# First key and value projections of a two-layer diffusion trunk: which engine makes the low weight parts, and in which order the opening steps stand

## The chip, the cores and the metric

The kernel runs on one core of one Trainium2 chip. A core has five engines with queues of their own: TensorE (PE in the profile, with PEld for its weight loads), VectorE (DVE), ScalarE (ACT), GpSimd (POOL) and SyncE (SP), which here issues nearly all DMA transfers. Engines wait for each other through semaphores; each works its own queue in order. The metric is the device time of one execution in microseconds (us), as the median of several runs.

## The reference

Two trunk layers work on 512 latent tokens of width 1024, with 256 context tokens beside them. What the change touches is the very beginning of layer 0:

```python
sh1, sc1, g1, sh2, sc2, g2 = adaln_params(c, mod_w[i], mod_b[i])         # silu(c) @ w + bias
h  = modulate(rms_norm(x,   norm_g[i, 0]), sh1,  sc1)                    # h * (1 + scale) + shift
hc = modulate(rms_norm(ctx, norm_g[i, 0]), csh1, csc1)
proj = h @ w_in                                                          # queries, keys and values
k_ac, v_ac, k_bc, v_bc = split_kv(hc @ w_in[:, Q_WIDTH:])
```

After that come global and windowed attention, a gated feed-forward part with a width-3 convolution, and a second layer with Fourier mixing in place of attention. All of it is float32.

## The kernel before, in words

**Products.** A float32 product is made of three faster ones. Every operand is split into a high part (a rounded copy, by ACT) and a low part (the operand less its high part), and `mm3` (lines 103 to 107) adds high times high (line 104), high times low (line 105) and low times high (line 106). `split` (line 126) makes the two parts of a weight; ACT's copy and the subtraction both carry line 127. In `split` the engine of the subtraction is an argument, VectorE if none is given.

**The opening.** The first 512 columns of the key and value weights (`w_kva`) are multiplied with all tokens: four latent token tiles and two context tiles of 128, each with an accumulator of its own. The width of 1024 is cut into eight chunks `c` of 128. For each chunk three things must be there before its products: the shift and scale of these 128 features (an adaLN tile), the split weights of the chunk, and the normalised tokens.

**The steps.** The order in which the code writes these steps is a string, `START` (line 60), which a loop walks through. Its letters are:

- `Mc`, `mod_tile(c)` (line 664): eight small float32 products with the adaLN weights of chunk c (line 672), ACT's copy of the sums (line 675), two transposes by TensorE (line 679), and three small VectorE steps (lines 681, 683, 685) that leave shift (`modc`) and scale (`derc`). The weights of all eight tiles are loaded by SP early on, into buffers that later hold other things (`yT`, `K`, `V` and a `raw` buffer).
- `Wc`, `weights(c)` (line 744): the split of the key and value weights of chunk c, 128x512 each. Two chunks share a load (`raw<-in_w_kva`, line 136) and a pair of buffers `wh`, `wl`. Before the change it passes GpSimd to `split`.
- `Xi` and `Y2`: sums of squares for the second half of the latent tokens (two parts) and for the context tokens (line 698 on VectorE, line 700 on ACT, products at line 187). `bcast` and `R2` (line 233) spread the reciprocal roots over the partitions; those of the second token half go inside `M2`.
- `Fci`, `feed(c, i)` (line 711): modulates chunk c of token set i (0 and 1 are the halves of the latent tokens, 2 is the context) and multiplies it with the weights, two token tiles with three products each. VectorE makes `md_t` (line 250), ACT the high part `hh` or `ch` (line 251), VectorE the low part `hl` or `cl` (line 252).
- `B0`, and part of `F01`: products by `busy` (line 179, product at line 181) whose result nobody reads. How many is set by the list `HOT` (line 56). In `F01` (lines 725 to 739) the products are written out on lines 737, 738 and 740, with `HOT[2]` busy products ahead of them and `HOT[3]` between their two parts.

**Who sets the order.** The string gives the order of the code; a scheduler with priorities then decides the order on each engine, so instructions of neighbouring steps are mixed. Weight loads share three `raw` buffers: SP may issue the next load into a buffer only when the low part made from it is done.

**What follows.** Three groups of further projections (`group_weights`, 128x1024 splits on VectorE, lines 104 to 106 with 128x256 results) run while VectorE and GpSimd normalise and rotate the keys and VectorE sums up two more adaLN rows (line 521). Then attention begins.

Of the kernel before, what the change touches and what calls it, by code (L numbers as in the profile page):

```python
# [10 lines left out]
F32 = mybir.dt.float32  # L11
# [41 lines left out]
SIDE = 16  # L53

WARM = 36
HOT = [5, 8, 5, 6]
HOT2 = [2, 2, 2]


START = ("M0 W0 X0 M1 B0 W1 F00 X1 F10 M2 W2 M3 F01 F11 F20 W3 F21 M4 Y2 F30 F31 R2 F02 W4 F12 F22 F32 M5 W5 F40 "  # L60
         "F41 M6 F42 W6 F50 F52 W7 F60 M7 F62 F51 F61 F70 F71 F72")

FILL = [[1, 0, 1, 2, 1, 1, 1, 1],
# [18 lines left out]
def kernel(ctx: ExitStack, tc: tile.TileContext, a):  # L82
    nc = tc.nc
    V, S, G, PE, SY = nc.vector, nc.scalar, nc.gpsimd, nc.tensor, nc.sync
# [15 lines left out]
    def f(ap):  # L100
        return ap.bitcast(F32)
# [19 lines left out]
    def held(i):  # L121
        if i.ins.engine in fences:
            tc.add_manual_dep(i.ins, fences[i.ins.engine], mybir.DependencyInfo(
                mybir.DependencyClass.NoSync, mybir.DependencyReason.DATA), reason="fence")

    def split(h, l, src, eng=V):
        i = S.copy(out=h, in_=src), eng.tensor_tensor(out=l, in0=src, in1=f(h), op=ALU.subtract)  # L127
        for j in i:
            held(j)
# [9 lines left out]
    def wpair(shape):  # L139
        return mk(wp, shape, F32R, "wh", 5), mk(wp, shape, F32R, "wl", 5)  # L140
# [35 lines left out]
    W4 = HT // 4  # L176


    def busy(ps, src, n):
        for _ in range(n):  # L180
            PE.matmul(ps[:32, :src.shape[1]], lhsT=ones32, rhs=src, start=True, stop=True)
# [396 lines left out]
    with ExitStack() as es:  # L578
# [27 lines left out]
        with ExitStack() as e1:  # L606
# [19 lines left out]
            kva = {}  # L626
# [64 lines left out]
            def x_sums(src, n, eng=V, hot=0, ps=None, ks=range(KC)):  # L691
                if ps is None:
                    ps = mk(pps, [P, T], F32, "mm", 6)
                for k in ks:
                    sq = sqx[:, nsq[0] % 6, :]
                    nsq[0] += 1
                    if k % 2:
                        eng.tensor_tensor(out=sq[:, :n], in0=src[:, k, :], in1=src[:, k, :], op=ALU.mult)
                    else:
                        i = S.activation(out=sq[:, :n], in_=src[:, k, :], func=AF.Square)  # L700
                        if nsq[0] == 1:
                            follow(i, ahead)
                    stat_add(ps, sq, n, k == 0, k == KC - 1)
                busy(warm, sq[:, :n], hot)
                return ps
# [10 lines left out]
            def feed(c, i):  # L716
# [12 lines left out]
                if (c, i) == (0, 1):  # L729

                    busy(warm, Rs[1], HOT[2])
                    for part in range(2):
# [8 lines left out]
                        if part == 0:  # L741
                            busy(warm, f(hh[:, 0, halves[1]]), HOT[3])

            def weights(c):
                if c % 2 == 0:
                    kw[c // 2] = wpair([P, 2, T])
                wh, wl = kw[c // 2]
                split(wh[:, c % 2, :], wl[:, c % 2, :], kva[c // 2][:, c % 2, :], G)

            ps0 = x_sums(xT[:, :, halves[0]], HT, V, HOT[0])  # L750

# [6 lines left out]

            for s in START.split():
                n = [int(c) for c in s[1:]]  # L760
                if s == "M0":
                    mod_tile(0, lambda: bcast(0, ps0))
                elif s == "M2":
                    mod_tile(2, lambda: bcast(1, Rs[1]))
                elif s == "Y2":
                    r2 = rstd(x_sums(cT, TC)[:, :W4])
                elif s == "R2":
                    Rs[2] = spread(r2, pps)
                elif s == "B0":
                    busy(warm, Rs[0], HOT[1])  # L770
                else:
                    {"M": mod_tile, "W": weights, "X": sums, "F": feed}[s[0]](*n)
# [489 lines left out]
    def ffn(l, xp, ready, pre, mid, gem, plain=None):  # L1262
# [146 lines left out]
        for gi, (f0, nch) in enumerate(GROUPS[l]):  # L1409
# [42 lines left out]
            for d in range(2):  # L1452
                weights(d)
# [3 lines left out]
            for d in range(KC):  # L1457
                if d not in ws:
                    weights(d)
                part(d, hs[d], begun.get(d))  # L1460
                if gem is not None and not end:
                    pump(gem, GP[1])
# [16 lines left out]
    with ExitStack() as es:  # L1479
        up = es.enter_context(tc.tile_pool(name="up", bufs=1, reuse_waits="tile", side="right"))  # L1480
        M1 = 258
# [104 lines left out]
        def fourier_weights(d, eng=G):  # L1586
            r = f_first[d] if d < 2 else raw([P, 4, 2, P], a["w_f"][d])

            pm = (yT[:, 6:8, :] if d in (3, 5) else yT[:, 2:4, :] if d == 1 else mk(cp, [P, 2, T], F32, "gacc")).rearrange(
                "p a (g c) -> p a g c", g=4)  # L1590
            held(eng.tensor_tensor(out=pm[:, 0, :, :], in0=r[:, :, 0, :], in1=r[:, :, 1, :], op=ALU.add))
            held(V.tensor_tensor(out=pm[:, 1, :, :], in0=r[:, :, 1, :], in1=r[:, :, 0, :], op=ALU.subtract))
            wh, wl = wpair([P, 2, 4, P])
            split(wh, wl, pm)
            return wh, wl
# [40 lines left out]
        for d in range(KC):  # L1636
            wh, wl = w_f.pop() if w_f else fourier_weights(d)
# [139 lines left out]
```

## Time and profile before

| what | value |
|---|---|
| median of 3 runs | 1136.24 us (1133.64 to 1137.02) |
| profiled execution | 1138.32 us, of which 1136.5 us are its span |
| PE busy | 1098.6 us, 97% of the span |
| DVE, ACT, POOL busy | 902.6, 592.9, 174.9 us |
| DMA from 10 to 40 us | 413 to 420 GB/s, busy share 1.01 to 1.04 |

The span runs from the first to the last instruction; the execution's own time is 1.8 us longer. In the timeline a row gives start, duration, engine, line, operation, tiles and count; what stands in square brackets is the idle time of the engine ahead of the row, and what ended it. A float32 product of lines 181, 187, 672 or 679 appears as two records, so that x10 at line 181 is five products.

### The profile page before, as it was taken

Reading aid. Unit: us, or ns where it says so; the run is one execution under the profiler, and the core shown is the slowest. Engines: PE = TensorE matmul, PEld = TensorE weight load, DVE = VectorE, ACT = ScalarE, POOL = GpSimd, SP = SyncE. Lnnn points to the kernel's source line nnn. Section 1 sums busy time; section 2 is a strip of 40 time slices with the busy share of each in tenths; the row PEclk is TensorE's granted clock in tenths of the full one; section 3 lists DMA queues with packets and bytes.
Section 4 is the critical chain, followed back from the end, with each engine's and each line's share of the span. In section 5 each row is a group of like instructions: output and inputs, shape, how many; then the busy total and the mean of one; then the engine's idle time right before and its main releaser. Section 6 shows DMA issues by size and latency. Waiting matters only on the chain.

```text
span 1136.5 us, 19542 instructions
## 1 busy us (share of the span) xinstructions
PE 1098.6 (97%) x7810; PEld 962.9 (85%) x7810; DVE 902.6 (79%) x1469; ACT 592.9 (52%) x1056; POOL 174.9 (15%) x180
## 2 busy tenths in 40 slices
PE   9999899999999999999999999889999999999995
PEld 5689888868898978887998998779888898899995
DVE  5678777773789976978998568878997998879755
ACT  4342355665665633552555446557745555555543
POOL 1136422422320000000000153610000000000012
PEclk9999999999999999999999999899999999999998
DMA  9676101174142455536425302732114523222332
GB/s 365 262 238 216 38 1 39 53 274 156 63 162 111 156 204 203 181 131 236 187 75 204 103 20 75 206 114 108 74 47 160 192 103 116 103 89 95 105 144 75
DMA packets 33764, 155.83 MB, mean 137 GB/s; under 512 B 3461, under 2 KB 8197, under 8 KB 22025
## 3 DMA queue, kind: packets, MB, share of 16 engines
q1 hardware_dynamic: 32520, 150.39, 36.8%
q0 software_dynamic: 1152, 4.19, 1.6%
q8 instruction: 61, 1.00, 0.3%
q14 instruction: 31, 0.25, 0.1%
HBM read 148.28 MB, written 6.29 MB: 136 GB/s over the span
## 4 chain that ended last, share of the span: by engine, by line
PE 73%; DVE 15%; ACT 5%; DMA 3%; issue 2%; POOL 1%; SPq 0%; DVEq 0%; POOLq 0%; ACTq 0%
PE mm L104 21%; PE mm L106 20%; PE mm L105 20%; DVE wl L127 2%; DVE md_t L317 2%; PE PT L969 1%; ACT wh L127 1%; PE gm L104 1%; PE O L105 1%; DMA raw<-in_w_up 1%; PE gm L106 1%; PE gm L105 1%; ACT hh L251 1%; PE O L104 1%; DVE cv L1286 1%
## 5 line engine op out<-in xcount | busy, mean ns | idle before, releaser
L127 ACT CAST wh<-raw 128x1024 fp32r<-128x1024 f32 (+2 forms) x207 | 190.6, 933 | 168.8 <-PE mm L105 113.0
L127 DVE TENSOR_TENSOR wl<-raw,wh 128x1024 fp32r<-128x1024 f32 (+2 forms) x197 | 214.6, 1097 | 52.2 <-ACT wh L127 51.9
L104 PE MATMUL mm<-hh,wh 128*128 128x256 f32 (+1 forms) x632 | 204.5, 324 | 3.0 <-ACT sq L1224 1.5
L106 PE MATMUL mm<-hh,wl 128*128 128x256 f32 (+1 forms) x632 | 202.1, 320 | 0.4 <-DVE wl L127 0.2
L105 PE MATMUL mm<-hl,wh 128*128 128x256 f32 (+1 forms) x632 | 201.5, 319 | 0.0
L292 POOL TENSOR_TENSOR gacc<-gacc,sq 128x256 f32<-128x256 f32 (+1 forms) x33 | 28.0, 848 | 715.3 <-ACT sq L290 714.6
L104 PEld LDWEIGHTS mm<-hh,wh 128*128 128x128 f32 x632 | 118.6, 188 | 17.6 <-ACT sq L1224 5.6
L106 PEld LDWEIGHTS mm<-hh,wl 128*128 128x128 f32 x632 | 118.6, 188 | 10.6 <-DVE wl L127 1.0
L105 PEld LDWEIGHTS mm<-hl,wh 128*128 128x128 f32 x632 | 118.7, 188 | 9.9
L104 PE MATMUL mm<-zh,wh 128*128 128x256 f32 x384 | 109.5, 285 | 1.5 <-ACT sq L1227 0.9
L104 PE MATMUL mm<-xh,wh 128*128 128x512 f32 (+1 forms) x302 | 107.1, 355 | 0.0
L106 PE MATMUL mm<-zh,wl 128*128 128x256 f32 x384 | 107.1, 279 | 0.0
L105 PE MATMUL mm<-zl,wh 128*128 128x256 f32 x384 | 107.0, 279 | 0.0
L105 PE MATMUL mm<-xl,wh 128*128 128x512 f32 (+1 forms) x302 | 106.5, 353 | 0.0
L106 PE MATMUL mm<-xh,wl 128*128 128x512 f32 (+1 forms) x302 | 106.2, 352 | 0.0
L104 PEld LDWEIGHTS mm<-zh,wh 128*128 128x128 f32 x384 | 72.1, 188 | 5.8 <-ACT sq L1227 4.4
L106 PEld LDWEIGHTS mm<-zh,wl 128*128 128x128 f32 x384 | 72.5, 189 | 0.0
L105 PEld LDWEIGHTS mm<-zl,wh 128*128 128x128 f32 x384 | 72.1, 188 | 0.0
L104 PEld LDWEIGHTS mm<-xh,wh 128*128 128x128 f32 x302 | 56.7, 188 | 9.4 <-issue 1.6
L105 PEld LDWEIGHTS mm<-xl,wh 128*128 128x128 f32 x302 | 56.7, 188 | 8.5 <-issue 0.4
L106 PEld LDWEIGHTS mm<-xh,wl 128*128 128x128 f32 x302 | 56.8, 188 | 8.1
L1285 ACT ACTIVATE cv<-mm,cols 128x512 f32<-128x512 f32 x59 | 45.7, 777 | 23.8 <-PE mm L106 17.6
(435 smaller groups left out, 2793.8 us busy)
## 6 DMA issues: line engine op xcount, KB each, us to landing
raw<-in_w_up SPq DMA_DIRECT2D x42, 1024.0 KB, 4.9
xT<-in_mod_r SPq DMA_DIRECT2D x20, 1024.0 KB, 5.0
raw<-in_w_down SPq DMA_DIRECT2D x32, 384.0 KB, 3.0
raw<-in_mod_p SPq DMA_DIRECT2D x8, 1024.0 KB, 4.9
raw<-in_w_down SPq DMA_DIRECT2D x16, 512.0 KB, 3.9
raw<-in_w_in SPq DMA_DIRECT2D x6, 1024.0 KB, 8.1
yT<-in_mod_r SPq DMA_DIRECT2D x10, 512.0 KB, 6.4
raw<-in_w_out SPq DMA_DIRECT2D x4, 1024.0 KB, 5.4
```

What stands on the lines that cost most here:

```text
L104: i = PE.matmul(out, lhsT=ah, rhs=bh, start=start, stop=False, skip_group_check=skip)
L105: PE.matmul(out, lhsT=ah, rhs=bl, start=False, stop=False, skip_group_check=skip)
L106: return i, PE.matmul(out, lhsT=al, rhs=bh, start=False, stop=stop, skip_group_check=skip)
L127: i = S.copy(out=h, in_=src), eng.tensor_tensor(out=l, in0=src, in1=f(h), op=ALU.subtract)
L251: S.activation(out=h, in_=t, func=AF.Identity, bias=bm, scale=1.0)
L292: G.tensor_tensor(out=self.acc[:, sl], in0=self.acc[:, sl], in1=sq[:, sl], op=ALU.add)
L317: m = V.scalar_tensor_tensor(out=t, in0=yT[:, k, hs], scalar=der[:, l, gi, k:k + 1], in1=R, op0=ALU.mult, op1=ALU.mult)
L969: PE.transpose(out=pt[:, j * P:(j + 1) * P], in_=Ps[j][:, off:off + P], identity=ident)
L1285: S.activation(out=cv, in_=ps, func=AF.Identity, bias=bc, scale=wc[1])
L1286: V.scalar_tensor_tensor(out=cv[:, 1:], in0=ps[:, :T - 1], scalar=wc[0], in1=cv[:, 1:], op0=ALU.mult, op1=ALU.add)
```

## The change

```diff
-HOT = [5, 8, 5, 6]
+HOT = [5, 8, 5, 0]
...
-START = ("M0 W0 X0 M1 B0 W1 F00 X1 F10 M2 W2 M3 F01 F11 F20 W3 F21 M4 Y2 F30 F31 R2 F02 W4 F12 F22 F32 M5 W5 F40 "
+START = ("M0 W0 X0 M1 B0 W1 F00 X1 F10 M2 F01 W2 F11 F20 M3 Y2 W3 F21 M4 R2 F30 F31 F02 W4 F12 F22 F32 M5 W5 F40 "
          "F41 M6 F42 W6 F50 F52 W7 F60 M7 F62 F51 F61 F70 F71 F72")
...
-                split(wh[:, c % 2, :], wl[:, c % 2, :], kva[c // 2][:, c % 2, :], G)
+                split(wh[:, c % 2, :], wl[:, c % 2, :], kva[c // 2][:, c % 2, :])
```

The eight subtractions of `weights` go from GpSimd to VectorE. `HOT[3]` goes from 6 to 0, so the six busy products inside `F01` are no longer issued. In `START`, `F01` stands ahead of `W2` and `M3`; `M3` stands behind `F20`, with `Y2` right behind it and ahead of `M4`; `R2` stands ahead of `F30` and no longer behind `F31`. SP's loads keep their order up to the third projection group's; each load that waited for a low part on GpSimd now waits for the same one on VectorE.

The first place is TensorE's queue from `F01` on. `mm_399` and `mm_400` (now `mm_379` and `mm_380`) are the accumulators of the second token half, `misc_379` before is `M3`'s result, `mm_133` takes the busy products. Before:

```order
L737 MATMUL mm_399<-wh_253,hh_69 128x512
L738 MATMUL mm_399<-wl_254,hh_69 128x512
L737 MATMUL mm_400<-wh_253,hh_69 128x512
L672 MATMUL misc_379<-yT_68,spad_170 32x256 x8
L738 MATMUL mm_400<-wl_254,hh_69 128x512
L181 MATMUL mm_133<-hh_69,ones_8_71 32x256
L679 MATMUL misc_379<-con_66,sq_388 128x128 x2
L181 MATMUL mm_133<-hh_69,ones_8_71 32x256 x5
L740 MATMUL mm_399<-wh_253,hl_70 128x512
L740 MATMUL mm_400<-wh_253,hl_70 128x512
```

TensorE's queue at the same place now, with the first product of `F11` as its last row:

```order
L737 MATMUL mm_379<-wh_253,hh_69 128x512
L738 MATMUL mm_379<-wl_254,hh_69 128x512
L737 MATMUL mm_380<-wh_253,hh_69 128x512
L738 MATMUL mm_380<-wl_254,hh_69 128x512
L740 MATMUL mm_379<-wh_253,hl_70 128x512
L740 MATMUL mm_380<-wh_253,hl_70 128x512
L104 MATMUL mm_379<-wh_253,hh_69 128x512
```

The six busy products are gone and `M3` with its transposes has left `F01`; it now stands behind `F20`, followed by the products of `Y2`.

The second place is VectorE's queue behind `M2`, where the second pair of weights is split. `md_t` and `hl` are the steps of `F01`, `F11`, `F20` and `F21`. Before:

```order
L683 TENSOR_TENSOR modc_173<-modc_173,cols_64 128x4
L250 SCALAR_TENSOR_TENSOR md_t_418<-xT_67,derc_174,Rs_365 128x256
L685 TENSOR_SCALAR derc_174<-modc_173,cols_64 128x2
L250 SCALAR_TENSOR_TENSOR md_t_428<-xT_67,derc_174,Rs_243 128x256
L252 SCALAR_TENSOR_TENSOR hl_70<-md_t_395,modc_173,hh_69 128x256
L252 SCALAR_TENSOR_TENSOR hl_70<-md_t_418,modc_173,hh_69 128x256
L252 SCALAR_TENSOR_TENSOR hl_70<-md_t_428,modc_173,hh_69 128x256
L250 SCALAR_TENSOR_TENSOR md_t_440<-xT_67,derc_174,Rs_365 128x256
L252 SCALAR_TENSOR_TENSOR hl_70<-md_t_440,modc_173,hh_69 128x256
```

VectorE's queue there now, where `wl_393<-raw_115` are the low parts of chunks 2 and 3:

```order
L683 TENSOR_TENSOR modc_173<-modc_173,cols_64 128x4
L250 SCALAR_TENSOR_TENSOR md_t_396<-xT_67,derc_174,Rs_365 128x256
L685 TENSOR_SCALAR derc_174<-modc_173,cols_64 128x2
L127 TENSOR_TENSOR wl_393<-raw_115,wh_392 128x512
L252 SCALAR_TENSOR_TENSOR hl_70<-md_t_375,modc_173,hh_69 128x256
L252 SCALAR_TENSOR_TENSOR hl_70<-md_t_396,modc_173,hh_69 128x256
L250 SCALAR_TENSOR_TENSOR md_t_406<-xT_67,derc_174,Rs_243 128x256
L127 TENSOR_TENSOR wl_393<-raw_115,wh_392 128x512
L250 SCALAR_TENSOR_TENSOR md_t_483<-xT_67,derc_174,Rs_365 128x256
L252 SCALAR_TENSOR_TENSOR hl_70<-md_t_406,modc_173,hh_69 128x256
L252 SCALAR_TENSOR_TENSOR hl_70<-md_t_483,modc_173,hh_69 128x256
```

The two subtractions stand among the steps of these four blocks; before, they stood in GpSimd's queue.

The third place is VectorE's queue around `M7`, the last adaLN tile, ahead of the last three blocks. `wl_857` and `wl_861` (now `wl_851` and `wl_855`) are the low parts of the first weights of the next stage, `md_t_732` (now `md_t_726`) belongs to `F70`. Before:

```order
L127 TENSOR_TENSOR wl_857<-raw_854,wh_856 128x1024
L127 TENSOR_TENSOR wl_861<-raw_854,wh_860 128x1024
L681 TENSOR_REDUCE modc_173<-misc_686 128x4
L252 SCALAR_TENSOR_TENSOR hl_70<-md_t_722,modc_173,hh_69 128x256
L683 TENSOR_TENSOR modc_173<-modc_173,cols_64 128x4
L685 TENSOR_SCALAR derc_174<-modc_173,cols_64 128x2
L250 SCALAR_TENSOR_TENSOR md_t_732<-xT_67,derc_174,Rs_243 128x256
```

VectorE's queue around `M7` now:

```order
L127 TENSOR_TENSOR wl_851<-raw_848,wh_850 128x1024
L681 TENSOR_REDUCE modc_173<-misc_680 128x4
L127 TENSOR_TENSOR wl_855<-raw_848,wh_854 128x1024
L683 TENSOR_TENSOR modc_173<-modc_173,cols_64 128x4
L685 TENSOR_SCALAR derc_174<-modc_173,cols_64 128x2
L250 SCALAR_TENSOR_TENSOR md_t_726<-xT_67,derc_174,Rs_243 128x256
```

The second large subtraction now stands inside `M7`'s three small steps, and the `hl` of `F61` has moved ahead of both. From row 236 of 6953 on TensorE's queue is the same as before.

## The prediction

> **What bounds the kernel now.** I read the page, its chain of waits, then the timeline of the opening, the only place where TensorE's queue differs between the two programs.
>
> ```profile
> span 1136.5 us, 19542 instructions
> PE 1098.6 (97%) x7810; PEld 962.9 (85%) x7810; DVE 902.6 (79%) x1469; ACT 592.9 (52%) x1056; POOL 174.9 (15%) x180
> PE 73%; DVE 15%; ACT 5%; DMA 3%; issue 2%; POOL 1%; SPq 0%; DVEq 0%; POOLq 0%; ACTq 0%
> ```
>
> TensorE works 97% of the span, and three quarters of the chain that ends last are its own. So the change is worth what it takes out of TensorE's queue, waits included. Busy time by stretch (length, then PE, PEld, DVE, ACT, POOL with counts, granted clock, DMA share, GB/s):
>
> ```profile
> 24.00:34.00 10.00, 8.98 (x50) 4.39 (x50) 8.96 (x21) 5.72 (x15) 2.81 (x2) 1.00 1.02 422
> 34.00:44.00 10.00, 9.77 (x117) 7.13 (x116) 2.22 (x9) 1.50 (x4) 2.54 (x2) 1.00 1.03 415
> 44.00:62.20 18.20, 17.46 (x98) 12.38 (x97) 17.22 (x35) 9.40 (x20) 2.78 (x2) 1.00 0.38 122
> 62.20:118.00 55.80, 55.79 (x461) 52.32 (x461) 43.88 (x75) 19.35 (x36) 31.53 (x29) 1.00 0.62 208
> ```
>
> From 62.2 to 118 us TensorE never stops: a lead won before is still there at 118, if what feeds TensorE moves along. Before 62.2 it stops now and then, and some of what it does is filler:
>
> ```profile
> 26.46 0.51 PE L737 MATMUL mm<-wh,hh 128*128 128x512 f32 x1
> 28.35 0.50 PE L738 MATMUL mm<-wl,hh 128*128 128x512 f32 x1
> 28.77 0.62 PE L181 MATMUL mm<-hh,ones 128*32 128x256 f32 x2
> 30.25 0.44 PE L679 MATMUL misc<-con,sq 128*128 128x128 f32 x2 [0.86 <-ACT sq L675]
> 30.62 2.35 PE L181 MATMUL mm<-hh,ones 128*32 128x256 f32 x10
> 32.89 0.73 PE L740 MATMUL mm<-wh,hl 128*128 128x512 f32 x2
> 39.37 0.44 PE L679 MATMUL misc<-con,sq 128*128 128x128 f32 x2 [0.23 <-ACT sq L675]
> 51.08 0.50 PE L106 MATMUL mm<-wh,cl 128*128 128x512 f32 x1 [0.64 <-DVE cl L252]
> ```
>
> Who causes the waits of 0.86 and 0.64 us? GpSimd's and VectorE's rows of the same moments:
>
> ```profile
> 24.72 2.81 POOL L127 TENSOR_TENSOR wl<-raw,wh 128x512 fp32r<-128x512 f32 x2 [9.96 <-ACT wh L127]
> 25.08 1.24 DVE L685 TENSOR_SCALAR derc<-modc,cols 128x2 f32<-128x2 f32 x1
> 26.35 1.46 DVE L250 SCALAR_TENSOR_TENSOR md_t<-xT,derc,Rs 128x256 f32<-128x256 f32 x1
> 27.74 1.26 DVE L252 SCALAR_TENSOR_TENSOR hl<-md_t,modc,hh 128x256 fp32r<-128x256 f32 x3
> 47.16 2.78 POOL L127 TENSOR_TENSOR wl<-raw,wh 128x512 fp32r<-128x512 f32 x2 [10.56 <-ACT wh L127]
> 47.26 2.97 DVE L250 SCALAR_TENSOR_TENSOR md_t<-xT,derc,Rs 128x256 f32<-128x256 f32 x2
> 58.11 0.23 DVE L685 TENSOR_SCALAR derc<-modc,cols 128x2 f32<-128x2 f32 x1
> 65.43 0.88 DVE L250 SCALAR_TENSOR_TENSOR md_t<-xT,derc,Rs 128x256 f32<-128x256 f32 x2
> ```
>
> While GpSimd subtracts, a `derc` of 0.23 us takes 1.24, and an `md_t` pair of 0.88 takes 2.97; the single `md_t` takes 1.46. Behind the first two wait ACT's `hh` and ACT's copy for `M3` (the 0.86 us); behind the pair waits the context's `cl` (the 0.64 us).
>
> **The change part by part.**
>
> *Busy products.* Would TensorE wait there anyway? `L740` needs `hl` of `F01`, which is made by 29.0 (27.74 and 1.26 for three); it starts at 32.89, right behind the filler. So the filler is on the path. From 28.77 to the transposes at 30.25 are 1.48 us (one product and the 0.86 us behind it); the other five take 30.62 to 32.89, 2.27 us. `M3` moves behind `F20`, where its transposes no longer stand between TensorE and work that is ready. Sum: 3.75 us gone.
>
> *Subtractions on VectorE.* The operation is in the trace on VectorE, with the same shape and operands, in later stages:
>
> ```profile
> L127 DVE TENSOR_TENSOR wl<-raw,wh 128x512 fp32r<-128x512 f32 x32 | 21.9, 685 | 4.5 <-ACT wh L127 4.5
> ```
>
> Eight of them add 8 x 0.685 = 5.5 us to VectorE, 0.60 each where steps follow closely (steps overlap by 0.08: three `hl` of 0.48 take 1.26). Out go the hold-ups: 1.01 (`derc`), 0.98 (`md_t`), 2.09 (the pair); VectorE's load grows by 1.4 us or less. Does a subtraction now stand ahead of something TensorE needs? I follow both queues to the tightest places.
>
> ```profile
> 37.75 1.07 PE L672 MATMUL misc<-K,spad 128*32 128x256 f32 x16
> 40.54 0.50 PE L104 MATMUL mm<-wh,hh 128*128 128x512 f32 x1
> 43.45 0.59 PE L233 MATMUL misc<-Rs,con 128*128 128x256 f32 x2
> 41.02 0.23 DVE L206 TENSOR_SCALAR st_v<-mm 128x64 f32<-128x64 f32 x1 [0.47 <-ACT st_r L205]
> 41.93 0.43 DVE L230 TENSOR_TENSOR Rs<-st_v,con 128x256 f32<-128x256 f32 x1
> 57.71 0.17 DVE L681 TENSOR_REDUCE modc<-misc 128x4 f32<-128x16 f32 x1
> ```
>
> TensorE: `F30` and `F31` took 40.54 to 43.45, so a block takes 1.45 us. `F01` begins at 26.46, `F11` at 27.9, `F20` at 29.4, `M3` at 30.8. An adaLN tile with `Y2` took 37.75 to 40.54, 2.8 us, its transposes ending after 2.06: 32.9 and 33.6. Then `F21` to 35.1, `M4` to 36.1, and `F30`, `F31` with `R2` (0.59) and two transposes (0.44) to 40.0; the third product of `F02`, which needs `cl`, comes at 40.6. VectorE: from `M3`'s transposes at 32.9 it has two adaLN triples of 0.63 (57.71 to 58.34), eight `md_t`, `hl` and `cl` of 0.40, the context's five steps (41.02 to 42.36) and two subtractions of 0.60: 1.3 + 3.2 + 1.3 + 1.2 = 7.0, so `cl` is there at 39.9. Margin 0.7 us; the 0.64 us wait goes.
>
> The other tight place is `F70`, where a large subtraction now stands inside `M7`'s steps:
>
> ```profile
> 61.17 2.36 DVE L127 TENSOR_TENSOR wl<-raw,wh 128x1024 fp32r<-128x1024 f32 x2
> 66.62 0.87 DVE L252 SCALAR_TENSOR_TENSOR hl<-md_t,modc,hh 128x256 fp32r<-128x256 f32 x2
> 68.18 0.39 PE L106 MATMUL mm<-wh,hl 128*128 128x512 f32 x1
> ```
>
> `hl` was there at 67.1 for a product at 68.18, margin 1.1. The subtraction takes 1.13 of it (2.36 for two, one of them 1.22), the `hl` of `F61` that left the place gives 0.40 back: some 0.35 stays.
>
> *Order.* What waits anew? `M4`'s weights in `K`:
>
> ```profile
> 15.44 0.33 SPq L624 DMA_DIRECT2D K<-in_mod_s  x1
> K<-in_mod_s SPq DMA_DIRECT2D x1, 1024.0 KB, 13.8
> ```
>
> They land at 29.2 and are now wanted at 35.1 and not 37.75: covered by 5.9 us, and the one tile that is wanted earlier. The load behind `W2`'s subtraction (the last key and value weights) is issued when `wl` is done, by my count 27.7 against 27.53 on GpSimd, so what is queued behind it on SP moves by 0.2. The 0.23 us ahead of the transposes moves with `Y2` to `M3`; I cost that at nothing. `R2` and `M4`'s transposes now cut `F30` in two places: a product behind such a cut takes 0.50 (28.35) instead of 0.39 (68.18). Against the two cuts that leave `F01` I take two more, 0.2 us lost.
>
> *Sum.* 3.75 + 0.64 - 0.2 = 4.2 us gained. Bounds: if both waits (1.5 us) return elsewhere, 2.7; if the 0.2 us and the 0.23 us fall away too, 4.6. I take 4.2, for the margins above are positive. The profiled execution, 1138.32 us with a span of 1136.5, would become 1134.1 and 1132.3. It lies 2.1 us above the median of the three runs, so the forecast is 1136.24 - 4.2 = 1132.0.
>
> **The rivals.**
>
> *The wait moves to VectorE (chance 0.22).* For it: VectorE is busy 17.22 of 18.20 us from 44 on, and the margins are 0.7 and 0.35. If each of the two subtractions ahead of `F02` cost what GpSimd needed (2.81 for two) and not 1.2, VectorE would be 1.6 late there, 0.9 beyond the margin; with as much at `F70`, 1.5 us or so return: 1133.5. The same time comes from another place:
>
> ```profile
> 97.82 13.25 POOL L851 TENSOR_SCALAR K<-K,krs 128x128 f32<-128x128 f32 x12 [4.58 <-DVE krs L167]
> 112.72 0.63 PE L597 MATMUL misc<-con,K 128*128 128x128 f32 x4
> ```
>
> The key transposes need eleven of GpSimd's twelve scalings, done at 110.0, 2.7 us ahead. If GpSimd did not start earlier, 1.5 of the 4.2 would go there. Against it: its chain starts from TensorE's own first results.
>
> *The filler was free (0.04).* If TensorE had to wait for `hl` anyway, only the waits of 1.5 us go, less 0.2: 1134.9. The 3.9 us between `hl` and `L740` speak against it.
>
> *Half clock (0.05, slower).* [...]
>
> ```profile
> 754.79 0.65 PE L187 MATMUL mm<-sq,ones 128*32 128x64 f32 x16 [1.88 <-ACT sq L196]
> 754.80:758.20 3.40, 3.40 (x42) 2.83 (x42) 3.40 (x11) 1.87 (x4) 0.00 (x0) 0.50 0.02 5
> ```
>
> Behind a wait of 1.88 us the granted clock was 0.50 for 3.4 us, which costs 1.7. Without filler, a tile that lands late leaves TensorE idle. The place is `M4`: if its weights landed at 39.3 and not 29.2, TensorE would stand 4.2 us and then run two such stretches at half clock, 3.4 us. That eats 7.6 of 4.2: 1139.6. Any landing after 35.1 begins to cost; from about 38 on the gain is gone. DMA is busy throughout (share 1.02), but nothing in the change delays this load. [...]
>
> **How the numbers follow.** The forecast has 0.69. A measurement of this kernel tells about 0.3% from no change, 3.4 us, so faster means below 1132.8. Which waits fall to half clock may differ from run to run, by 1.7 us a stretch; that alone can bring 4.2 under 3.4, for which I take 0.11 off the forecast, and it can lift 0.05 of the other cases over it. Faster 0.63; same 0.32; slower 0.05. The range goes from 4.6 gained with one such stretch less (1129.9) to the rival at 1134.9.
>
> **What would show it.** In the changed profile: no line 181 between 27 and 60 us; no VectorE step of lines 250 or 685 over 0.6 us before 60; GpSimd idle from its first memsets to the keys; TensorE's waits between 24 and 62 under 0.6 us together; `M7`'s products (62.20 before) near 58.0, the key transposes near 108.5. I am wrong if `M7` is early but the transposes are not, if a wait for `cl`, `hl` or a weight tile of over 0.5 us stands in the opening, or if the clock there is below 1.00.

## The result, and the profile after

The changed kernel takes 1128.86 us (median of 6 runs, 1127.52 to 1129.85), the kernel before 1135.65 in the same count. The ratio is 0.9938 with an interval of 0.9925 to 0.9950: 6.8 to 7.0 us faster, where 4.2 were forecast and the range ended at 1129.9. The direction was right and the size was not. A second timing gave 1128.22 against 1135.02, ratio 0.9940 (0.9927 to 0.9953). One of the six executions of run e11 below took 3928.76 us and is not in its ratio; the median of its other five is 1129.44.

The head of the page, as the prediction showed it of before (span, TensorE's share, the chain that ended last by engine):

```profile
span 1126.2 us, 19518 instructions
PE 1093.7 (97%) x7798; PEld 960.3 (85%) x7798; DVE 902.4 (80%) x1477; ACT 593.6 (53%) x1056; POOL 165.1 (15%) x172
PE 77%; DVE 13%; ACT 5%; DMA 2%; issue 1%; POOL 1%; POOLq 0%; DVEq 0%; ACTq 0%
```

TensorE is still the bound, with twelve records fewer. Its rows of the opening:

```profile
22.33 1.07 PE L672 MATMUL misc<-yT,spad 128*32 128x256 f32 x16
...
26.77 0.51 PE L737 MATMUL mm<-wh,hh 128*128 128x512 f32 x1
...
27.81 0.63 PE L740 MATMUL mm<-wh,hl 128*128 128x512 f32 x2
...
32.73 0.44 PE L679 MATMUL misc<-con,sq 128*128 128x128 f32 x2 [0.18 <-ACT sq L675]
...
40.54 0.40 PE L106 MATMUL mm<-wh,cl 128*128 128x512 f32 x1
...
56.88 0.64 PE L672 MATMUL misc<-K,spad 128*32 128x256 f32 x8
...
66.67 0.28 PE L104 MATMUL mm<-wh,hh 128*128 128x256 f32 x1
...
107.09 0.38 PE L597 MATMUL misc<-con,K 128*128 128x128 f32 x2
```

`F01`'s two parts follow each other without filler (the second starts at 27.81, where 32.89 stood), the wait of 0.86 is gone, the product that needs `cl` runs without a wait, and `M7` begins at 56.88 and not 62.20. The key transposes are 5.1 us early (107.09, before 112.20), so the lead lasts into attention. VectorE's rows beside it:

```profile
25.39 0.22 DVE L685 TENSOR_SCALAR derc<-modc,cols 128x2 f32<-128x2 f32 x1
25.52 0.68 DVE L127 TENSOR_TENSOR wl<-raw,wh 128x512 fp32r<-128x512 f32 x1
...
26.91 0.48 DVE L250 SCALAR_TENSOR_TENSOR md_t<-xT,derc,Rs 128x256 f32<-128x256 f32 x1
...
39.48 1.27 DVE L252 SCALAR_TENSOR_TENSOR cl<-md_t,modc,ch 128x256 fp32r<-128x256 f32 x3
```

The `derc` that took 1.24 us takes 0.22, the `md_t` of 1.46 takes 0.48; the subtraction costs 0.68. The first `cl` is made about 0.6 us ahead of its product at 40.54, which is the margin that was forecast (0.7).

**How the opening is measured below.** From the first product of `M2`'s tile (22.33 above) to the first 128x256 product (66.67 above) the changed kernel takes 44.34 us. The kernel before:

```profile
22.02 1.07 PE L672 MATMUL misc<-yT,spad 128*32 128x256 f32 x16
...
71.89 0.28 PE L104 MATMUL mm<-wh,hh 128*128 128x256 f32 x1
```

49.87 us. The lead in the opening is 5.53 us. All leads are in us against this kernel; to line 482, a place some 25 us further on that the expectations use, the changed kernel's is 5.52.

### The profile page after: what moved, and what is told of

Read it like the earlier page. It is cut to its first block, busy times and chain, and to the rows that moved or that the text cites. A ratio compares the mean times of both kernels' runs of the same rounds, so it can differ in the third digit from the quotient of the medians.

```text
span 1126.2 us, 19518 instructions
## 1 busy us (share of the span) xinstructions
PE 1093.7 (97%) x7798; PEld 960.3 (85%) x7798; DVE 902.4 (80%) x1477; ACT 593.6 (53%) x1056; POOL 165.1 (15%) x172
## 4 chain that ended last, share of the span: by engine, by line
PE 77%; DVE 13%; ACT 5%; DMA 2%; issue 1%; POOL 1%; POOLq 0%; DVEq 0%; ACTq 0%
PE mm L104 22%; PE mm L106 21%; PE mm L105 20%; DVE wl L127 2%; DMA raw<-in_w_up 2%; DVE md_t L317 1%; PE PT L969 1%; ACT wh L127 1%; PE O L105 1%; PE gm L104 1%; PE O L104 1%; PE gm L106 1%; PE gm L105 1%; ACT hh L251 1%; PE O L106 1%
## 5 line engine op out<-in xcount | busy, mean ns | idle before, releaser
L127 DVE TENSOR_TENSOR wl<-raw,wh 128x1024 fp32r<-128x1024 f32 (+2 forms) x205 | 220.8, 1085 | 54.4 <-ACT wh L127 54.2
```

## The experiments

The ratio is not the quotient of the two medians; for e2 that quotient (0.9972) lies at the edge of the interval.

| run | what it is | opening | lead | median, and before on the same chip | ratio (interval) |
|---|---|---|---|---|---|
| e1 | subtractions on VectorE alone | 48.14 | 1.73 | 1133.97, 1136.00 | 0.9983 (0.9974 to 0.9992) |
| e2 | busy products dropped alone | 47.58 | 2.29 | 1132.78, 1136.00 | 0.9982 (0.9972 to 0.9992) |
| e3 | new order alone | 49.48 | 0.39 | 1135.73, 1136.00 | 1.0004 (0.9993 to 1.0015) |
| e4 | all but the order | 45.79 | 4.08 | 1131.54, 1136.00 | 0.9966 (0.9954 to 0.9978) |
| e5 | all but the subtractions | 46.59 | 3.28 | 1132.46, 1135.76 | 0.9973 (0.9963 to 0.9984) |
| e6 | all but the dropped products | 47.26 | 2.61 | 1132.60, 1135.76 | 0.9980 (0.9971 to 0.9990) |
| e7 | changed, filler ahead of `F01` dropped too | 44.98 | 4.89 | 1131.48, 1135.76 | 0.9957 (0.9945 to 0.9970) |
| e8 | before, a second trace | 49.88 | 0 | one run: 1136.37 | |
| e9 | changed, again | 44.33 | 5.54 | 1128.22, 1135.02 | 0.9940 (0.9927 to 0.9953) |
| e10 | `M3`'s products in the wait ahead of `F01` | 43.62 | 6.25 | 1128.06, 1135.02 | 0.9936 (0.9924 to 0.9947) |
| e11 | the same without filler | 43.25 | 6.62 | 1129.92, 1135.02 | 0.9950 (0.9937 to 0.9964) |
| e12 | e10 with `M7` in one piece | 42.95 | 6.92 | 1127.08, 1134.06 | 0.9938 (0.9924 to 0.9952) |
| e13 | changed, opening made late by filler | 49.59 | 0.28 | 1134.12, 1134.06 | 1.0001 (0.9992 to 1.0010) |

**The parts alone and in pairs (e1 to e6).** The edits are the three hunks of the change, alone or left out:

```diff
 # e1: the subtractions alone
-                split(wh[:, c % 2, :], wl[:, c % 2, :], kva[c // 2][:, c % 2, :], G)
+                split(wh[:, c % 2, :], wl[:, c % 2, :], kva[c // 2][:, c % 2, :])
 # e2: the busy products alone
-HOT = [5, 8, 5, 6]
+HOT = [5, 8, 5, 0]
 # e3: the new START alone; e4, e5, e6: the changed kernel with the old START, with G, with HOT[3] = 6
```

> Before with one part of the change: the low parts of the key and value weights on VectorE. The opening is read from the first product of F01 to the first product of line 482; it took 70.00 us before and 64.48 after, a lead of 5.52. Theory A (each wait that GpSimd's subtractions cause is on TensorE's path): the 0.86 us ahead of M3's transposes and the wait for cl go, and so does the wait for the context's high part that only the weight loads show (0.58 on their row at 45.56): opening about 68.0, lead 2.0, median about 1133.7. Rival B (the waits come back elsewhere, since VectorE now does the subtractions): lead under 0.5. Rival C (a part of the measured 6.8 us is not in the opening but in stretches at half clock, which fall by chance): the median then differs from 1135.7 minus the lead by up to 1.7 us a stretch, in either direction, in every kernel of this row.

Measured: 68.92 us to line 482, a lead of 1.08, and 1.73 at the first 128x256 product. The two differ because the stretch between those places takes 24.57 or 25.21 us in two executions of the same kernel (e8 below); all leads here are therefore read at the 128x256 product. The waits of 0.86 and 0.64 us are gone, and nothing came back: A, but for its third wait. The one for the context's high part `ch` is still there, on the weight load's row of e1, with its 0.58 us, so GpSimd did not cause it:

```profile
44.80 0.19 PEld L104 LDWEIGHTS mm<-wh,ch 128*128 128x128 f32 x1 [0.58 <-ACT ch L251]
```

> Before with one part: the six busy products of F01 dropped. Theory A: the five products behind M3's transposes are on the path (2.27 us), the one ahead of them lies in the 0.86 us wait, which stays and grows to 1.3; the scheduler no longer puts four of M6's products ahead of F02, which gives some 0.5: lead 2.3 to 2.8, median about 1133.2. If the filler was free: lead under 0.6. If the wait for cl grows by what TensorE is early (its chain on VectorE begins with M4's transposes, which move along, so I do not expect it): lead under 1.5.

Measured: 2.28 to line 482, 2.29 here. The filler was on the path: the stops in `F01` shrink by 2.9 us, more than the five products' 2.27, since its last two products now run in the wait ahead of the transposes (0.93). But the total is a sum of other things too. The wait for `cl` is gone (0.9), while the step with `R2`, which now waits 0.47 for VectorE, grows by 0.7, `M7`'s sixteen products are cut into ten and six, which costs about 0.7, and 0.2 go at `M6`'s transposes. That 2.29 stands beside the 2.27 of the sum is luck. `M6`'s four products no longer stand ahead of `F02`, and the 0.5 us expected for that did not come: `R2` to `F02`'s first product takes 2.20 us, and took 2.11.

> Before with one part: the new order of the blocks, filler and GpSimd as before. Theory A: M3 leaves F01's stretch, so the 0.86 us wait and the cuts around it go, but all six busy products stay on the path; M4 in its new place costs what M3 cost there less 0.4; M6's early products are together again (0.5): lead 1.4 to 2.0, with the wait for cl (0.64) still there, median about 1134. If the order alone did nothing: lead under 0.4. If GpSimd's subtractions now hold up F11 (its low parts of the activations come from VectorE at 28.97 in the changed kernel, just in time): lead 0 or below.

Measured: 70.26 us to line 482 (0.26 late), 0.39 early at the 128x256 product, and no gain in time. I had the right kind of rival and the wrong place. GpSimd's rows, VectorE's and TensorE's around `M3` and `Y2` in e3:

```profile
36.33 2.53 POOL L127 TENSOR_TENSOR wl<-raw,wh 128x512 fp32r<-128x512 f32 x2 [8.63 <-ACT wh L127]
36.44 0.17 DVE L681 TENSOR_REDUCE modc<-misc 128x4 f32<-128x16 f32 x1 [0.73 <-ACT wh L127]
36.65 0.99 DVE L683 TENSOR_TENSOR modc<-modc,cols 128x4 f32<-128x4 f32 x1
37.67 1.22 DVE L685 TENSOR_SCALAR derc<-modc,cols 128x2 f32<-128x2 f32 x1
...
40.01 0.49 PE L104 MATMUL mm<-wh,hh 128*128 128x512 f32 x1 [0.69 <-ACT hh L251]
...
41.74 0.45 PE L233 MATMUL misc<-Rs,con 128*128 128x256 f32 x1 [1.25 <-DVE Rs L230]
```

The new order puts GpSimd's pair of subtractions on top of `M3`'s small steps. Two steps that took 0.16 and 0.23 us in before (57.91 and 58.11) take 0.99 and 1.22, and each ends within 0.05 us of one of GpSimd's operations (half of 2.53 us after 36.33, and at 38.86). TensorE then waits 0.69 and 1.25 us, which eats what the order wins. The reduction beside them, at 36.44, was not held: 0.17 us, as at 57.71 in before. Why it was not, and the two steps were, is not shown.

> The changed kernel with the old order of the blocks (subtractions on VectorE, no filler). Theory A: 5.52 less what the order gives with the others in place: M3's sixteen products, its transposes and two cuts stand in F01's stretch again, against M4's in F30: about 0.8, lead 4.5 to 5.0. If the order carries most of the gain (more than 2): lead under 3.5. If it carries nothing: lead 5.4 or more.

Measured: 4.06 to line 482 and 4.08 here, so the order is worth 1.45 with the other parts in place, more than I expected. TensorE's rows of e4 show its two largest costs, the wait for `ch` behind `R2` (0.52 on TensorE's own row, 0.50 by what follows below) and `M7` cut into ten and six products (about 0.7). The second stands in neither the kernel before nor the changed one:

```profile
39.31 0.60 PE L233 MATMUL misc<-Rs,con 128*128 128x256 f32 x2
39.84 1.07 PE L672 MATMUL misc<-V,spad 128*32 128x256 f32 x16
41.43 0.50 PE L104 MATMUL mm<-wh,ch 128*128 128x512 f32 x1 [0.52 <-ACT ch L251]
...
56.40 0.59 PE L672 MATMUL misc<-V,spad 128*32 128x256 f32 x2
...
58.52 0.63 PE L672 MATMUL misc<-V,spad 128*32 128x256 f32 x6
```

> The changed kernel with the subtractions back on GpSimd (new order, no filler). Theory D, formed on the row of the order alone (lead -0.26): there GpSimd's pair of subtractions at 36.33 falls on VectorE's steps for M3's tile and the context's statistics, a derc takes 1.22, and TensorE waits 0.69 for F30 and 1.25 for R2; so the new order needs VectorE's subtractions. Then the same two waits stand here, and without filler TensorE also waits for the low parts of F01, which VectorE has at 29.1 there: lead 1.2 to 2.5 of 5.52, no matter that two of the three parts are in. Theory A (parts add up, with little between them): 5.52 - 1.08 = 4.4.

Measured: 2.63 to line 482, 3.28 here. The waits of D are there, at a different size: `F01` waits 0.60 us for `hl`, `R2` 1.13 for a step that takes 0.42 in the changed kernel (36.20; GpSimd's, VectorE's and TensorE's rows of e5):

```profile
36.86 2.74 POOL L127 TENSOR_TENSOR wl<-raw,wh 128x512 fp32r<-128x512 f32 x2 [9.40 <-ACT wh L127]
37.09 1.38 DVE L230 TENSOR_TENSOR Rs<-st_v,con 128x256 f32<-128x256 f32 x1
38.62 0.67 PE L233 MATMUL misc<-Rs,con 128*128 128x256 f32 x2 [1.13 <-DVE Rs L230]
```

`F30`'s wait is not there, so the loss against the changed kernel is 2.25 us and not 3.0 to 4.3.

> The changed kernel with the six busy products back in F01 (twelve matmuls in the records). Theory A: the low parts of F01 are there at 27.0 (26.12 and 0.87), the first product that reads them would start at 27.81, so all twelve at about 0.23 each lie on the path: lead 5.52 - 2.8 = 2.7. If the filler were covered by something behind it (VectorE's row ends with F11's last low part at 28.78, just when its product starts, so F11 can't wait for filler): lead over 4.

Measured: 2.61 (1.96 to line 482). All twelve matmuls are on the path: A.

Put together, the totals of the subtractions and the filler add up (1.73 + 2.29 = 4.02, measured 4.08), though not place by place: the wait for `cl` goes in e1 and again in e2, and could go only once. The order is worth 0.39 alone, 0.88 with the subtractions, 0.99 with the filler gone and 1.45 with both.

**The filler ahead of `F01` dropped too (e7).**

```diff
-HOT = [5, 8, 5, 0]
+HOT = [5, 8, 0, 0]
```

> The changed kernel without the filler ahead of F01 as well (ten matmuls, 24.49 to 26.77). Theory E (there VectorE is the bound: it works without a gap from 24.43 to 29.4, and F11's last low part is ready at 28.78, when its product starts): F01 starts when its high parts are made, about 25.9, 0.9 earlier, but F11 then waits 0.8 for its low parts, and the lead stays 5.4 to 5.8. If filler there was still on the path: lead 6.3. Rival clock (filler is what keeps the clock up): TensorE stands still for some 1.4 us ahead of F01, a stretch at half clock follows in the opening, and the lead falls to 4 or below.

Measured: the rival; 65.95 us from `F01` to line 482, a lead of 4.05. TensorE's rows of e7, then its busy time by stretch (length, then PE, PEld, DVE, ACT, POOL with counts, granted clock, DMA share, GB/s):

```profile
25.73 0.56 PE L737 MATMUL mm<-wh,hh 128*128 128x512 f32 x1 [1.60 <-ACT hh L251]
26.09 0.63 PE L738 MATMUL mm<-wl,hh 128*128 128x512 f32 x1
26.52 0.63 PE L737 MATMUL mm<-wh,hh 128*128 128x512 f32 x1
```

```profile
22.60:26.00 3.40, 1.80 (x17) 0.88 (x10) 1.77 (x7) 2.51 (x6) 0.00 (x0) 1.00 1.03 423
26.00:29.40 3.40, 3.40 (x9) 2.66 (x9) 3.22 (x9) 1.76 (x6) 0.00 (x0) 0.51 1.03 424
```

After a wait of 1.60 us the clock is 0.51 for 3.4 us, and a product every 0.43 us replaces one every 0.23. `F01` starts 0.8 us earlier, and the opening is still 0.64 longer than the changed kernel's. So the half clock that the prediction feared exists in the opening. It came when the five products ahead of `F01` went (0.51); when the change dropped the six inside `F01`, the clock stayed at 1.00 (22.3 to 66.7 us of the changed kernel).

**Before once more (e8).** No edit.

> The kernel before, unchanged, for a second trace of it: it tells which differences between the two first traces are those of one execution. Expected from the queue alone: the opening again 70.0 within 0.1, with the same waits (0.86 for M3's transposes, 0.64 for cl), while the stretches at half clock lie elsewhere or are fewer than the three of the first trace (713.8, 717.2 and 754.8 us), and the span with them is shorter by some 1.7 us a stretch. If the opening itself differs by over 0.5, the lead of 5.52 is uncertain by as much.

Measured: the same to the first 128x256 product (49.88), with the waits at 0.84 and 0.62. To line 482 it is 70.65 and not 70.00. The difference is one of pace, over products that need nothing new. TensorE in 12 us of before, then of e8:

```profile
71.90:83.90 12.00, 12.00 (x107) 12.00 (x106) 8.30 (x13) 2.62 (x6) 8.95 (x10) 1.00 0.75 268
```

```profile
72.30:84.30 12.00, 12.00 (x104) 12.00 (x103) 8.35 (x13) 2.56 (x6) 8.95 (x10) 1.00 0.75 272
```

107 products against 104, at the same granted clock. The half clock was not in its place: the first trace has two such stretches from 713.8 us on, this one none there (clock 1.00 from 714 to 721 us), and a span 1.9 us shorter.

**The changed kernel once more (e9).** No edit.

> The changed kernel, unchanged, timed again on a chip together with the kernel before. From the first product of M2's tile to the first 128x256 product TensorE took 49.87 us in the two traces of before and 44.34 in the changed kernel's: 5.53 less, while the first median stood 6.8 to 7.0 below that of before, from six runs. If the excess of about 1.4 is the chance of few runs and of stretches at half clock, the median comes out 5.5 to 6.3 below that of before, and this opening is 44.3 within 0.1 again. If something behind the opening also gains: 6.8 or more below, with the opening the same.

Measured: opening 44.33, and the median again 6.8 below that of before. The opening explains 5.5; the interval (5.3 to 8.3 us) takes that in, but in both timings the medians differ by 1.3 us more. By what was expected, 6.8 speaks for something behind the opening; e13 speaks against it.

**A better order (e10 to e12).** `M3`'s sixteen products go ahead of `F01`, where TensorE waits for VectorE; e11 drops the rest of the filler there, e12 keeps `M7` together by putting it behind `F60`. In the code `P3` is `mod_tile(3)` up to its products, and `follow` sets the order of two instructions of one engine.

```diff
-HOT = [5, 8, 5, 0]
+HOT = [5, 8, 2, 0]          # e11: [5, 8, 0, 0]
-... F10 M2 F01 W2 F11 F20 M3 Y2 ...
+... F10 M2 P3 F01 W2 F11 F20 M3 Y2 ...
 # e12, in mod_tile, first product of M7:
+                            follow(i, early_ps["F60"])
```

> The changed kernel with M3's sixteen products put where busy products stand ahead of F01 (its weights land at 24.2 us; M3's copy, transposes and VectorE steps stay behind F20), and busy products there cut from ten matmuls to four. A stop of TensorE for sixteen such products costs 1.09 whatever stands around it, and ahead of F01 TensorE waits for VectorE anyway: 1.1 us less than the changed kernel, opening 43.2, median about 1128. No half clock in the opening, since TensorE is kept busy but for some 0.3 us. Rival: in this order R2 stands behind two subtractions on VectorE, and waits there; then 0.5 or less is left.

Measured: 43.62, 0.7 better and not 1.1. `R2` did not wait; `M7` was cut in two as in e4.

> The same with no busy product ahead of F01. VectorE is the bound there (F11's last low part was ready just when its product started), so F01 starts earlier by up to 0.9 but F11 waits for it: opening within 0.3 of the kernel with four. Clock: without any filler (the row without busy products ahead of F01) TensorE stood still for 1.60 us, and the next stretch of 3.4 us ran at half clock, which cost 1.7 of its lead; here M3's products fill 1.1 of that wait, so I expect 1.00 throughout the opening. If half clock shows here too, 1.7 is lost.

Measured: 43.25, 0.37 below e10. No half clock shows in the opening: from `F01` on (25.92 to 60.22 us) products with nothing between them follow each other every 0.22 to 0.24 us, where e7's took 0.43. The time is no better than e10's.

> The kernel with M3's products in the wait ahead of F01, and M7's sixteen products kept behind F60. In the kernel without this, M3's own stop was gone (1.09) and F01 came 0.4 earlier, but the scheduler cut M7 into ten and six products, which cost 1.07 and 0.66 instead of 1.09, so that the opening was 43.62 and not 42.9. If a tile in two pieces pays twice, as M6's four early products did in the kernel before: opening 42.9 to 43.0, 1.4 below the changed kernel's 44.33, median about 1127.3. If the second piece only fills a wait: opening 43.5 or more.

Measured: 42.95, as expected: the cut cost 0.67 us. TensorE's rows of e12 at `M7`:

```profile
55.80 0.64 PE L676 MATMUL misc<-K,spad 128*32 128x256 f32 x8
56.26 0.61 PE L676 MATMUL misc<-V,spad 128*32 128x256 f32 x8
```

It has the shortest opening of all, 1.4 us below the changed kernel's, and the lowest median. Its ratio to before (0.9938) can't be told from the changed kernel's (0.9940): the gain of e12 over it is shown in the opening alone.

**To whom the rest belongs (e13).** Twelve busy products more ahead of `F01`, so that what follows starts as late as before; the scheduler also moved some splits and a load of the next stage.

```diff
-HOT = [5, 8, 5, 0]
+HOT = [5, 8, 17, 0]
```

> The changed kernel with its opening made late: seventeen busy products instead of five ahead of F01, 24 matmuls more of 0.23 us, so that everything behind starts when it does in the kernel before (opening 49.9 against 49.87). The changed kernel's medians stood 6.8 to 6.9 us below before's, the opening 5.53; this tells to whom the other 1.3 us belong. If they belong to the order or to the subtractions (something behind the opening runs better for it): median still 1.0 to 1.4 below that of before. If they come from being early (or from chance): 0.4 or less below it.

Measured: 0.06 above the median of before, ratio 1.0001. Neither the order nor the subtractions win anything behind the opening that this interval (1.1 us to either side) could show.

## Why the prediction was wrong in size

**What held.** That the filler was on the path: put back into the changed kernel, its twelve matmuls cost 2.9 us (e6); e2's 2.29 beside the 2.27 of the sum is luck. The hold-ups on VectorE and who waits behind them (e1). The margins: no wait for `cl`, `hl` or a weight tile stands in the opening, and TensorE's waits from 24 to 62 us are 0.34 together (0.16 ahead of the filler, 0.18 at 32.73). No busy product stands between 27 and 60, no `md_t` or `derc` there takes over 0.6. The clock in the opening is 1.00 (22.3 to 66.7 us).

**The step that failed** is the sum "3.75 + 0.64 - 0.2". It put one term at nothing: the wait for `ch` behind `R2`, which the new order removes (0.50 us); of the order the sum holds only "Against the two cuts that leave `F01` I take two more, 0.2 us lost." And it took `F01`'s stop at 3.75 where 4.41 stood, and the wait for `cl` at 0.64 where 0.90 stood. I find the terms by one rule: projection products follow each other every 0.23 us (71.19, 71.42 and 71.65 in before), and whatever a step between two of them takes beyond that is the price of the stop between them. By this rule the opening's 133 projection products have 14.77 us of stops before and 9.27 after. TensorE's rows of before that the prediction did not read, and the weight load's row of the same moment:

```profile
43.97 1.07 PE L672 MATMUL misc<-V,spad 128*32 128x256 f32 x16
44.85 0.60 PE L672 MATMUL misc<-raw,spad 128*32 128x256 f32 x4
45.56 0.51 PE L104 MATMUL mm<-wh,ch 128*128 128x512 f32 x1
...
46.37 0.39 PE L106 MATMUL mm<-wh,cl 128*128 128x512 f32 x1
...
50.05 0.39 PE L105 MATMUL mm<-wl,ch 128*128 128x512 f32 x1
...
55.23 1.06 PE L672 MATMUL misc<-raw,spad 128*32 128x256 f32 x12
56.21 0.50 PE L104 MATMUL mm<-wh,ch 128*128 128x512 f32 x1
```

```profile
45.56 0.19 PEld L104 LDWEIGHTS mm<-wh,ch 128*128 128x128 f32 x1 [0.58 <-ACT ch L251]
```

The same places in the changed kernel, TensorE's rows:

```profile
36.49 0.50 PE L104 MATMUL mm<-wh,hh 128*128 128x512 f32 x1
36.83 0.61 PE L233 MATMUL misc<-Rs,con 128*128 128x256 f32 x2
37.09 0.58 PE L105 MATMUL mm<-wl,hh 128*128 128x512 f32 x1
37.51 0.38 PE L679 MATMUL misc<-con,sq 128*128 128x128 f32 x2
37.65 0.48 PE L106 MATMUL mm<-wh,hl 128*128 128x512 f32 x1
37.97 0.40 PE L104 MATMUL mm<-wh,hh 128*128 128x512 f32 x1
...
45.34 0.40 PE L106 MATMUL mm<-wh,cl 128*128 128x512 f32 x1
45.67 1.07 PE L672 MATMUL misc<-V,spad 128*32 128x256 f32 x16
46.67 0.50 PE L104 MATMUL mm<-wh,hh 128*128 128x512 f32 x1
```

| term | forecast | measured | from |
|---|---|---|---|
| `F01`'s stop | 3.75 | 4.41 | 28.35 to 32.89 is 4.31 beyond the pace, 0.10 behind it; gone now |
| `R2` and two transposes in their new place | -0.2 | -0.26 | `R2` took 0.52 (43.45 to 43.97); now both cuts together cost 0.78 (36.49 to 37.97, 1.48 for three steps) |
| the wait for `ch` behind `R2` | 0 | 0.50 | 43.97 to 45.56 is 1.59; `M5`'s sixteen alone cost 1.09 now (45.34 to 46.67, less 0.23) |
| the wait for `cl` | 0.64 | 0.90 | 50.05 to 51.08 less 0.23, and the next product 0.11 late |
| `M3` instead of `M4` with `Y2`, small rest | 0 | -0.05 | what is left of 14.77 - 9.27 |
| sum | 4.2 | 5.5 | lead 5.53 |

So two terms were too small, and one was missing. `F01`'s stop lacked the transposes' own 0.37 (30.25 to 30.62) and 0.29 around the busy products.

The missing term is a chain, not work of TensorE. Ahead of `F02`, `R2`'s product has to be copied by ACT, multiplied into `md_t` by VectorE and rounded to `ch` by ACT (at 44.07, 44.48 and 45.00 us before), and from that product to `F02`'s first pass 2.11 us before (43.45 to 45.56) and 2.12 in e4 (39.31 to 41.43). The four early products of `M6` stand in this stretch before and not in e4, so they fill a wait and cost nothing. Nor does `M6` gain by staying whole, for its other twelve took 0.98 (55.23 to 56.21) where sixteen take 1.00 in e4. The new order puts `R2` ahead of `F30`'s last products, 3.24 us ahead of `F02` (36.83 to 40.07), and the chain is covered. TensorE's idle column shows no such wait before, since `M6`'s products lie over it; the weight load's row does.

The prediction held a second road to a better figure and did not take it: its own timetable has `F02`'s third product 14.1 us behind `F01`'s first, and 13.8 were measured; before, the first product with `cl` (46.37) came 19.9 behind it. That is 5.8 less, of which 0.2 is one product more that stood ahead of it before and 1.1 come back later for `M5`'s tile, while 0.8 more go at the wait for `cl`: 5.3, nearer to 5.5 than the sum's 4.2.

**The rivals.** The wait did not move to VectorE: it would have, at `M3` and `R2`, had the order come without the subtractions (e3, e5); the prediction saw these two parts as independent. The filler was not free (e2, e6). Half clock did not come; it did when the filler just ahead of `F01` was dropped too (e7, 0.51 for 3.4 us). The 7.6 us of that rival rest on two such stretches behind a wait of 4.2 us, an estimate of mine: before has two on end (0.50 from 713.8 to 720.6 us), but ahead of them TensorE was busy for 2.43 of 3.41 us.

**What stays open.** The medians moved 6.8 to 7.0 us, the opening 5.5. TensorE's queue behind it is the same, and e13 leaves no room for more than some 1 us that order or subtractions win there. Being early could itself win something, but e12, with 1.4 us more lead, does not show it (6.98 by medians, lead 6.92). One of these stretches has two paces, and one kernel shows both (0.64 us, e8). Half clock comes and goes: between 700 and 760 us the first trace of before has three such stretches of 3.4 us (from 713.8, 717.2 and 754.8 us), its second trace none from 714 to 721, the first trace of the changed kernel one (from 747.2 us). By the ratios, time and lead agree within 0.9 us in e1 to e6 and e12; that the two timings of the changed kernel both fell 1.3 lower may be chance. It is not shown.

## What to carry to other kernels

Price a stop of the busiest engine by the step between its neighbours less their steady pace, not by its idle column: that finds waits that other work or a modelled end hides. When the scheduler's order changes, list which groups were split or joined, and ask of each whether its piece lies in a wait: the cut of `M7`'s sixteen products cost 0.67 us (e10 against e12), that of `M6`'s nothing. And try the parts apart before calling them independent: this order was worth 0.39 us alone and 1.45 with its companions. A total that fits can still hide two errors of opposite sign (e2).

## What the runs showed of the hardware

The granted clock halved for about 3.4 us at a time (0.50 in before, 0.51 in e7). TensorE was busy for 2.43 of the 3.41 us ahead of the first such stretch in before, and for 1.80 of 3.40 in e7. In before:

```profile
710.39:713.80 3.41, 2.43 (x14) 1.70 (x13) 3.41 (x8) 1.60 (x4) 3.41 (x4) 1.00 0.08 14
713.80:717.20 3.40, 3.40 (x16) 3.10 (x15) 3.00 (x5) 0.00 (x0) 2.96 (x3) 0.50 1.01 314
```

The place changes from one execution to the next: half clock from 713.80 us on in one trace of before, 1.00 from 714 to 721 in the other. The busy time of TensorE's rows ahead does not decide it alone: half clock followed the stretch above, busy for 2.43 of 3.41 us, while in the changed kernel the clock stayed at 1.00 behind one busy for 1.72 of 3.40 (115.70 to 119.10). What decides it was not found. And a chain of 128x256 products ran at 107 or at 104 in 12 us at clock 1.00, in two executions of one kernel; what decides between these was not found either.
